# Summing the modulation by rows of 1024 columns instead of 512, with the bias added at the way out of PSUM

## The chip, the cores and the metric

The kernel runs on one core of one Trainium2 chip, as one launch. The metric is the device time of that launch in microseconds (us). The core has five engines with instruction streams of their own: TensorE (PE; its weight loads are shown apart as PEld), VectorE (DVE), ScalarE (ACT), GpSimd (POOL) and SyncE (SP), which here issues nearly all DMAs. PSUM is the memory TensorE writes to; VectorE and ScalarE read results out of it, GpSimd cannot.

## What is computed

Two layers of a diffusion backbone over 512 latent tokens and 256 context tokens, width 1024, all float32. Each layer mixes tokens by three head groups (latent attention, differential attention, a Hyena convolution), then runs a squared-ReLU MLP of width 4096. Both sub-layers are modulated. For each layer the condition vectors are multiplied with a matrix of 1024 x 6144, and the result is cut into six kinds of 1024 numbers:

```
silu_c, silu_cc = jax.nn.silu(c), jax.nn.silu(c_ctx)          # two vectors of 1024
mod   = silu_c  @ w_mod[layer] + b_mod[layer]
mod_c = silu_cc @ w_mod[layer] + b_mod[layer]
sh1, sc1, g1, sh2, sc2, g2 = jnp.split(mod[:, None, :], 6, axis=-1)
px = (layer_norm(x) * (1 + sc1) + sh1) @ w_in[layer]
x  = post_norm(alpha * x + g1 * (ox @ w_out[layer] + b_out[layer]), ...)
x  = post_norm(alpha * x + g2 * ffn(layer_norm(x) * (1 + sc2) + sh2), ...)
```

Kinds 2 and 5 (g1, g2) are gates, one row over all tokens. Kinds 0, 1, 3, 4 are shifts and scales.

## The kernel before

The kernel splits each float32 operand of its large products into a high and a low part and runs three matmuls for each product (`mm3`, `split`). In the MLP, seven of eight blocks of 512 hidden units go through a seven-product (Strassen-like) scheme (`down7`), whose operands are sums made by VectorE or GpSimd and then split again.

Nothing is issued in the order of the program text. Every operation is first recorded as a task (`Plan.note`), with a cost from the kernel's own table (`cost`). `schedule` and `explore` then lay the tasks out in time: in steps of 12 us they try up to 10 orders, nine of them with random changes of the ranks, and keep the one that uses TensorE best over a look ahead. The result is one fixed order for each engine. Where an operation may go to several engines (`either`: `copy` and `scaled` to ScalarE or VectorE, `tt` to VectorE or GpSimd if both inputs are in SBUF, else to VectorE alone; `stt` is VectorE's alone), the planner picks. All instructions go out from line 856, so the profile has one line for everything and the groups are told apart by tile and shape.

SBUF is one arena of 784 units of 64 floats per partition (`S4`, tiles named slab_s in the profile), cut into parts of 16 units. A tile of 512 columns takes 8 units, one of 1024 a whole part. PSUM has eight banks of 512 floats (`mm`, ps_mm in the profile).

Of the twelve kinds of modulation in the two layers, four (layer 0: kinds 0, 1, 3, 4) are multiplied on TensorE by `mod`, which the change leaves alone. The other eight are made by `mod_sum`, without the large matmul: the eight row blocks of 128 rows of `w_mod` are loaded, each multiplied by one number per partition (`cs`, named cc in the profile) and added up in an accumulator of 128 partitions, and at the end a matmul with ones adds the 128 partitions. Layer 0's kinds 2 and 5 and layer 1's kinds 0 and 1 are made for both condition vectors (vs = 2), layer 1's kinds 2 to 5 for the latent tokens' vector alone (vs = 1). `WIDTH` says how many columns are done at a time: with 512, each kind is done in two halves, one after the other.

In each half, the first row block is written to the accumulator by `scaled`, and the bias, loaded to partition 0 alone, is added to partition 0 of it by a `tt` of one partition; the sum over partitions later carries it along. Of the seven other row blocks, those with k + v odd are one `stt` (multiply and add) on VectorE; the others are a `scaled` and a `tt`. At the end a gate's row of 2 x 512 leaves PSUM by `copy` and is written to DRAM (`grow`), to be read back when the gate is used; a shift or a scale lands transposed, 128 x 4 numbers a half, by a `tensor_scalar` into `modT`.

`sums` of layer 0's kind 2 is woven with the spectra of the convolution beside the first projections. The other seven are woven into layer 0's MLP (`RATIO_F`): kind 5 of layer 0 first, then the six of layer 1. Tasks of `mod_sum` are marked loose: the planner's window of 30 us of TensorE work does not wait for them.

Of the kernel before, what the change touches and what calls it, by code (L numbers as in the profile page):

```python
# [12 lines left out]
F32 = mybir.dt.float32  # L13
F32R = mybir.dt.float32r
AF = mybir.ActivationFunctionType
ALU = mybir.AluOpType
AX = mybir.AxisListType
P = 128
# [869 lines left out]
class Net:  # L888
# [7 lines left out]
    DOWN7 = (7, 7)  # L896
    HOT = 12
    UNITS = 784
    WIDTH = 512

    def __init__(self, ctx, tc, A, out):
        self.A, self.out = A, out
# [254 lines left out]
    def mod_sum(self, l, jj, vs):  # L1157

        nc, A = self.nc, self.A
        plan = self.plan  # L1160
        width = self.WIDTH
        n = D // width
        gate = jj in (2, 5)
        if gate:

            g = self.dp.tile([2, D], F32, name=f'grow_{l}_{jj}')
        else:

            t = self.const([P, 8, 2], f'modT_{l}_{jj}')
        for h in range(n):  # L1170
            plan.loose = True
            c0 = jj * D + h * width
            bias = self.S4(width, dt=F32)
            nc.sync.dma_start(out=bias[0:1, :], in_=A['b_mod'][l, c0:c0 + width].unsqueeze(0))
            acc = [self.S4(width, dt=F32) for _ in range(vs)]
            for k in range(8):
                plan.loose = True
                w = self.S4(width, dt=F32)
                nc.sync.dma_start(out=w, in_=A['w_mod'][l, k * P:(k + 1) * P, c0:c0 + width])
                for v in range(vs):  # L1180
                    c = self.cs[:, v, k:k + 1]
                    if k == 0:
                        self.scaled(acc[v], w, c)
                        self.tt(out=acc[v][0:1], in0=acc[v][0:1], in1=bias[0:1], op=ALU.add)
                    elif (k + v) % 2:
                        self.stt(out=acc[v], in0=w, scalar=c, in1=acc[v], op0=ALU.mult, op1=ALU.add)
                    else:
                        x = self.S4(width, dt=F32)
                        self.scaled(x, w, c)
                        self.tt(out=acc[v], in0=acc[v], in1=x, op=ALU.add)  # L1190
                plan.loose = False
                yield 1.0 / n
            plan.loose = True
            if gate:
                row = self.S4(width, dt=F32)
                for o in range(0, width, 512):
                    p = self.mm()
                    for v in range(vs):
                        s = self.pick[:, v] if vs == 2 else self.ones[:, 0:2]
                        nc.tensor.matmul(p[0:2], s, acc[v][:, o:o + 512], start=(v == 0), stop=(v == vs - 1))  # L1200
                    self.copy(row[0:2, o:o + 512], p[0:2])
                nc.sync.dma_start(out=g[:, h * width:(h + 1) * width], in_=row[0:2])
            else:
                m = width // P
                p = self.mm(vs, m, 2)
                for v in range(vs):
                    for k in range(m):
                        nc.tensor.matmul(p[:, v, k], acc[v][:, k * P:(k + 1) * P], self.ones[:, 0:2], start=True, stop=True)
                nc.vector.tensor_scalar(out=t[:, h * m:(h + 1) * m, 0:vs].rearrange('p k v -> p v k'), in0=p[:, :, :, 0],
                                        scalar1=1.0 if jj in (1, 4) else 0.0, scalar2=None, op0=ALU.add)  # L1210
            plan.loose = False
            yield 2.0 / n
        if gate:
            self.grow[l, jj] = g
        else:
            self.modT[l, jj] = t
# [1199 lines left out]
```

## Time and profile before

| | us |
|---|---|
| median of three runs | 1800.85 |
| lowest and highest run | 1797.39, 1802.88 |
| the profiled execution's own time | 1796.01 |
| its span, first to last instruction | 1794.2 |

The profiled execution shows, as shares of the span, PE busy 98%, PEld 83%, DVE 81%, ACT 62%, POOL 29%, with a granted TensorE clock of 0.999 of full speed. An engine's busy time says how long an instruction of its own was in flight. TensorE's matmuls overlap, so its busy time can be near the whole span while the matmuls still come further apart than they could.

### The profile page before, as it was taken

The page shows a single profiled execution, that of the slowest core. Times are in us where ns is not written, and L with a number is a line of the kernel's source. Part 1 is how long each engine was busy: PE and PEld are TensorE (multiplying, and loading weights), DVE is VectorE, ACT ScalarE, POOL GpSimd, SP SyncE. Part 2 cuts the span into 40 slices and gives each one's busy share as a digit, 9 for nine tenths or more (in the row PEclk, how much of TensorE's full clock was granted, in tenths as well). Part 3 has the DMA queues.
Part 4 walks back from the last instruction along what each step waited for, and adds up shares of the span by engine and source line. Part 5 has one row for each costly group of instructions (what it writes and reads, how often), then busy time and mean ns, then how long its engine had stood idle before and what let it go on. Part 6 is the DMA issues. An engine that isn't in the chain of part 4 may idle for free.

```text
span 1794.2 us, 27787 instructions
## 1 busy us (share of the span) xinstructions
PE 1757.7 (98%) x9706; PEld 1480.8 (83%) x9706; DVE 1448.4 (81%) x2554; ACT 1115.2 (62%) x2411; POOL 514.8 (29%) x584
## 2 busy tenths in 40 slices
PE   7999999999999999999999999999999999999997
PEld 2898888887788888887888788998988898888886
DVE  5988866688858999969787788567889788888888
ACT  5645767667828966555554448467679487555542
POOL 3342212174305104214312415012342421222230
PEclk9999999999999999999999999999999999999999
DMA  9497422272334444335334325531524242332251
GB/s 310 88 298 227 137 68 64 83 229 84 121 115 165 165 147 162 105 128 181 103 104 141 135 79 143 193 94 27 185 75 154 91 153 86 119 116 94 94 176 47
DMA packets 165128, 237.21 MB, mean 132 GB/s; under 512 B 36532, under 2 KB 107060, under 8 KB 164987
## 3 DMA queue, kind: packets, MB, share of 16 engines
q1 hardware_dynamic: 153787, 211.84, 36.4%
q0 software_dynamic: 11200, 23.60, 4.4%
q8 instruction: 76, 1.25, 0.3%
q14 instruction: 65, 0.53, 0.1%
HBM read 211.51 MB, written 23.89 MB: 131 GB/s over the span
## 4 chain that ended last, share of the span: by engine, by line
PE 77%; DVE 11%; ACT 6%; DMA 3%; issue 2%; POOL 1%; SPq 0%; POOLq 0%; ACTq 0%; DVEq 0%
PE ps_mm L856 77%; DVE slab_s L856 10%; ACT slab_s L856 6%; DVE st L856 1%; DMA slab_s<-w_mod 1%; DMA slab_s<-w_in 1%; DMA slab_s<-hy_fw 1%; POOL st L856 1%; DMA slab_s<-w_ff 0%; POOL slab_s L856 0%; DMA ident<-k_ident 0%; SPq L856 0%; POOLq L2412 0%; DVE modT L856 0%; ACTq L856 0%
## 5 line engine op out<-in xcount | busy, mean ns | idle before, releaser
L856 PE MATMUL ps_mm<-slab_s,slab_s 128*128 128x512 f32 (+7 forms) x8366 | 1624.5, 350 | 13.4 <-ACT slab_s L856 5.9
L856 PEld LDWEIGHTS ps_mm<-slab_s,slab_s 128*128 128x128 f32 (+3 forms) x8366 | 1353.1, 188 | 226.4 <-ACT slab_s L856 22.7
L856 DVE TENSOR_TENSOR slab_s<-slab_s,slab_s 128x512 fp32r<-128x512 f32 (+9 forms) x898 | 623.5, 736 | 118.0 <-ACT slab_s L856 87.5
L856 ACT CAST slab_s<-slab_s 128x512 fp32r<-128x512 f32 (+8 forms) x837 | 454.4, 581 | 226.1 <-DVE slab_s L856 67.8
L856 POOL TENSOR_TENSOR slab_s<-slab_s,slab_s 128x512 fp32r<-128x512 f32 (+9 forms) x258 | 330.8, 1288 | 793.5 <-DVE slab_s L856 342.3
L856 DVE TENSOR_TENSOR slab_s<-ps_mm,slab_s 128x512 f32<-128x512 f32 (+6 forms) x520 | 316.3, 629 | 85.4 <-PE ps_mm L856 50.2
L856 PE MATMUL ps_mm<-ident,slab_s 128*128 128x128 f32 (+3 forms) x1020 | 177.5, 273 | 7.1 <-ACT slab_s L856 4.6
L856 ACT COPY slab_s<-ps_mm 128x512 f32<-128x512 f32 (+6 forms) x229 | 109.8, 489 | 98.0 <-PE ps_mm L856 88.9
L856 ACT ACTIVATE slab_s<-ps_mm,b 128x256 f32<-128x256 f32 (+2 forms) x176 | 71.8, 450 | 144.2 <-PE ps_mm L856 140.6
L856 PEld LDWEIGHTS ps_mm<-ident,slab_s 128*128 128x128 f32 (+3 forms) x1020 | 122.9, 140 | 35.8 <-ACT slab_s L856 13.5
L856 ACT ACTIVATE slab_s<-ps_mm,st 128x768 f32<-128x768 f32 (+2 forms) x162 | 121.9, 762 | 38.0 <-DVE st L856 14.9
L856 DVE TENSOR_REDUCE st<-ps_mm 128x1 f32<-128x768 f32 (+1 forms) x140 | 117.4, 844 | 26.8 <-PE ps_mm L856 24.1
L856 ACT ACTIVATE slab_s<-slab_s,st 128x96 f32<-128x96 f32 (+2 forms) x86 | 64.1, 747 | 66.5 <-DVE st L856 62.4
L856 DVE SCALAR_TENSOR_TENSOR slab_s<-slab_s,st,slab_s 128x1024 f32<-128x1024 f32 (+3 forms) x84 | 92.0, 1097 | 11.1 <-ACT slab_s L856 6.1
L856 ACT ACTIVATE slab_s<-slab_s,cc 128x512 f32<-128x512 f32 x103 | 72.2, 722 | 20.2 <-DVE slab_s L856 12.2
L856 ACT ACTIVATE slab_s<-slab_s 128x256 f32<-128x256 f32 (+3 forms) x186 | 73.5, 435 | 17.3 <-DVE slab_s L856 16.6
L856 ACT CAST slab_s<-ps_mm 128x512 fp32r<-128x512 f32 (+5 forms) x145 | 70.7, 498 | 20.4 <-PE ps_mm L856 17.0
L856 POOL TENSOR_SCALAR st<-st 128x1 f32<-128x1 f32 (+2 forms) x55 | 23.9, 435 | 196.4 <-ACT slab_s L856 195.2
L856 DVE SCALAR_TENSOR_TENSOR slab_s<-slab_s,cc,slab_s 128x512 f32<-128x512 f32 x80 | 63.2, 803 | 3.1 <-POOL slab_s L856 2.7
L856 POOL TENSOR_TENSOR slab_s<-slab_s 128x256 f32<-128x256 f32 (+1 forms) x39 | 34.4, 890 | 99.8 <-DVE slab_s L856 74.2
L856 PE MATMUL ps_mm<-slab_s,cc 128*2 128x512 f32 x128 | 60.6, 592 | 2.3 <-DMA slab_s<-w_mod 2.3
L856 POOL TENSOR_TENSOR st<-st,mhalf 128x1 f32<-128x1 f32 (+2 forms) x59 | 48.2, 817 | 45.6 <-DVE st L856 41.5
(92 smaller groups left out, 660.6 us busy)
## 6 DMA issues: line engine op xcount, KB each, us to landing
slab_s<-w_ff SPq DMA_DIRECT2D x128, 512.0 KB
slab_s<-w_mod SPq DMA_DIRECT2D x128, 256.0 KB
slab_s<-w_mod SPq DMA_DIRECT2D x32, 512.0 KB
slab_s<-x SPq DMA_DIRECT2D x22, 512.0 KB
slab_s<-w_in SPq DMA_DIRECT2D x24, 384.0 KB
slab_s<-k_fw_l POOLq DMA_DIRECT2D x16, 512.0 KB, 5.3
slab_s<-k_iv_l POOLq DMA_DIRECT2D x16, 512.0 KB, 5.4
slab_s<-w_out SPq DMA_DIRECT2D x16, 512.0 KB
```

The source lines that it names most:

```text
L856: made[i] = f(*[put(v) for v in a], **{n: put(v) for n, v in k.items()})
```

## The change

`WIDTH` goes from 512 to 1024, so each of the eight kinds is done in one pass over whole rows. The bias is no longer added to partition 0 of the accumulator. It is loaded where the result needs it: for a gate on two partitions, 1024 numbers each, and added as the row leaves PSUM (a `tt` in place of `copy`); for a shift or scale as 128 x 8, eight numbers per partition, which are 1024 words of four bytes each from addresses that are 128 words apart along a partition, and added in the `stt` that replaces `tensor_scalar`.

```
-    WIDTH = 512
+    WIDTH = 1024
...
-            bias = self.S4(width, dt=F32)
-            nc.sync.dma_start(out=bias[0:1, :], in_=A['b_mod'][l, c0:c0 + width].unsqueeze(0))
+            b_mod = A['b_mod'][l, c0:c0 + width]
+            if gate:
+                bias = self.S4(width, dt=F32)
+                nc.sync.dma_start(out=bias[0:2, :], in_=b_mod.unsqueeze(0).to_broadcast([2, width]))
+            else:
+                bias = self.S4(width // P, dt=F32)
+                nc.sync.dma_start(out=bias, in_=b_mod.rearrange('(m p) -> p m', p=P))
...
                         self.scaled(acc[v], w, c)
-                        self.tt(out=acc[v][0:1], in0=acc[v][0:1], in1=bias[0:1], op=ALU.add)
...
-                    self.copy(row[0:2, o:o + 512], p[0:2])
+                    self.tt(out=row[0:2, o:o + 512], in0=p[0:2], in1=bias[0:2, o:o + 512], op=ALU.add)
...
-                nc.vector.tensor_scalar(out=t[:, h * m:(h + 1) * m, 0:vs].rearrange('p k v -> p v k'), in0=p[:, :, :, 0],
-                                        scalar1=1.0 if jj in (1, 4) else 0.0, scalar2=None, op0=ALU.add)
+                self.stt(out=t[:, h * m:(h + 1) * m, 0:vs].rearrange('p k v -> p v k'), in0=p[:, :, :, 0], scalar=1.0 if jj in (1, 4) else 0.0,
+                         in1=bias.unsqueeze(1).to_broadcast([P, vs, m]), op0=ALU.add, op1=ALU.add)
```

## Rows read from the trace of the kernel before

**Rows 1.** Windows of the whole core: busy time (instructions) of each engine, clock, DMA

```profile
535.00:960.00 425.00, 421.47 (x2252) 355.27 (x2251) 371.35 (x581) 265.88 (x569) 126.24 (x108) 1.00 0.43 143
140.00:200.00 60.00, 59.84 (x323) 49.99 (x322) 52.84 (x87) 38.24 (x71) 11.84 (x11) 1.00 0.74 229
1500.00:1750.00 250.00, 249.90 (x1098) 204.75 (x1097) 207.24 (x286) 133.03 (x269) 67.31 (x50) 1.00 0.36 116
```

**Rows 2.** Waits of TensorE from 535 to 960 us: total, times, longest

```profile
PE ps_mm L856 <- DVE slab_s L856: 1.8, 1, 1.8
PE ps_mm L856 <- ACT slab_s L856: 0.7, 1, 0.7
PE ps_mm L856 <- POOL slab_s L856: 0.3, 1, 0.3
```

**Rows 3.** The chain of waits, from 589 to 621 us

```profile
589.65 0.77 DVE slab_s L856 x2
...
590.48 2.18 DMA slab_s<-w_mod
592.66 0.63 DVE slab_s L856
...
596.56 8.64 DMA slab_s<-w_mod
605.22 3.56 DMA slab_s<-w_ff
...
609.26 3.46 DVE slab_s L856 x6
```

**Rows 4.** Groups by shape over the span: what the change touches, and nearest shapes

```profile
L856 DVE TENSOR_TENSOR slab_s<-slab_s,slab_s 128x512 f32<-128x512 f32 x190 | 135.2, 737 | 20.8 <-ACT slab_s L856 20.2
...
L856 ACT ACTIVATE slab_s<-slab_s,cc 128x512 f32<-128x512 f32 x103 | 72.2, 722 | 20.2 <-DVE slab_s L856 12.2 <-DMA slab_s<-w_mod 6.8 <-POOL slab_s L856 0.9
...
L856 DVE SCALAR_TENSOR_TENSOR slab_s<-slab_s,cc,slab_s 128x512 f32<-128x512 f32 x80 | 63.2, 803 | 3.1 <-POOL slab_s L856 2.7
...
L856 DVE SCALAR_TENSOR_TENSOR slab_s<-slab_s,st,slab_s 128x1024 f32<-128x1024 f32 x36 | 49.2, 1368 | 10.2 <-ACT slab_s L856 6.1 <-POOL st L856 3.6
L856 DVE SCALAR_TENSOR_TENSOR slab_s<-slab_s,slab_s 128x1024 f32<-128x1024 f32 x36 | 44.1, 1232 | 0.2
...
L856 ACT ACTIVATE slab_s<-slab_s,st 128x1024 f32<-128x1024 f32 x38 | 43.6, 1149 | 51.5 <-DVE st L856 50.5 <-DMA slab_s<-w_mod 0.4 <-PE ps_mm L856 0.3
...
L856 DVE TENSOR_TENSOR slab_s<-slab_s,slab_s 128x1024 f32<-128x1024 f32 x17 | 23.1, 1370 | 0.0
...
L856 DVE TENSOR_TENSOR slab_s<-slab_s,slab_s 1x512 f32<-1x512 f32 x18 | 13.3, 757 | 0.7 <-ACT slab_s L856 0.6
...
L856 ACT COPY slab_s<-ps_mm 2x512 f32<-2x512 f32 x15 | 8.6, 571 | 8.0 <-PE ps_mm L856 7.9
...
L856 DVE SCALAR_TENSOR_TENSOR slab_s<-slab_s,cc 128x512 f32<-128x512 f32 x8 | 6.7, 832 | 0.0
...
L856 POOL TENSOR_TENSOR slab_s<-slab_s,slab_s 1x512 f32<-1x512 f32 x6 | 7.7, 1279 | 5.8 <-DVE slab_s L856 2.9 <-ACT slab_s L856 2.1 <-issue 0.7
```

**Rows 5.** The same view, what reads PSUM on VectorE with a second operand

```profile
L856 DVE TENSOR_TENSOR slab_s<-ps_mm,slab_s 128x512 f32<-128x512 f32 x327 | 215.6, 682 | 56.0 <-PE ps_mm L856 50.2 <-ACT slab_s L856 2.4 <-DMA slab_s<-k_win_c 0.8
```

**Rows 6.** Tiles w_mod, b_mod and grow: issues, shortest/median/longest ns, first and last start

```profile
L856 SPq DMA_DIRECT2D slab_s<-w_mod x160: 327/368/1487, 1.9 to 953.5; - x160
...
L856 SPq DMA_DIRECT2D slab_s<-b_mod x20: 244/272/491, 3.0 to 944.1; - x20
...
L856 SPq DMA_DIRECT2D grow<-slab_s x8: 250/251/257, 172.3 to 1004.4; - x8
L856 SPq DMA_DIRECT2D slab_s<-grow x6: 326/339/459, 465.6 to 1714.5; - x6
```

**Rows 7.** Scattered loads: issue of MLP bias and convolution weights; then windows while they run

```profile
L856 SPq DMA_DIRECT2D b<-b_ff x2: 398/414/430, 62.8 to 1087.9; - x2
...
L856 SPq DMA_DIRECT2D cw<-hy_conv_w x2: 478/1621/2764, 42.4 to 1075.2; - x2
...
60.00:65.00 5.00, 5.00 (x31) 5.00 (x30) 4.97 (x14) 4.85 (x11) 0.00 (x0) 1.00 0.27 6
65.00:70.00 5.00, 5.00 (x25) 4.39 (x25) 4.60 (x10) 1.76 (x4) 2.75 (x5) 1.00 0.26 2
```

**Rows 8.** Matmuls by shape from 690 to 705 us, and from 1500 to 1750 us

```profile
L856 PE MATMUL ps_mm<-slab_s,slab_s 128*128 128x512 f32 x68 | 15.7, 391 | 0.0
...
L856 PE MATMUL ps_mm<-slab_s,slab_s 128*128 128x512 f32 x1098 | 250.5, 390 | 0.1
```

## The prediction

> **What bounds the kernel now.** I read the windows first, then TensorE's waits, then the chain of waits, and only then the prices of single instructions. The windows tell where the touched work lies. The sums load `w_mod` until 953.5 us [rows 6], in two stretches: 140 to 200 us (layer 0, kind 2) and 535 to 960 us (the other seven kinds). In the second TensorE is busy 421.47 of 425 us, in the first 59.84 of 60 [rows 1]. So all the time in which TensorE visibly stands still there is 3.53 + 0.16 = 3.7 us, 0.2% of the kernel. The reader should compare this with VectorE in the same row: 371.35 of 425, 87%, the fullest of the engines that feed TensorE. It is the one that the change relieves, and it is not the one that sets the end, except at a few places.
>
> Which places, the waits tell: from 535 to 960 us TensorE waited 1.8 us for VectorE, 0.7 for ScalarE, 0.3 for GpSimd [rows 2]. The chain of waits shows the worst one, at the start of layer 0's MLP: VectorE, then loads of `w_mod` (2.18 and 8.64 us), one of `w_ff` (3.56) and VectorE's splits again, up to 612.7 us [rows 3]. There the sums' work and the MLP's first weights compete.
>
> **The change, part by part.** A sum of one kind with two vectors has, per half, 2 `scaled` for the first block, 7 `stt`, and 7 `scaled` with 7 `tt`; with one vector 1, 4, 3 and 3. Four kinds of each sort in two halves make 88 `stt`, 104 `scaled` and 80 `tt`, and 24 adds on one partition. The rows have these counts: 80 + 8 `stt`, 103 `scaled` on ScalarE, 18 + 6 adds on one partition [rows 4]. With whole rows the first three halve, and the adds go.
>
> TensorE: the same matmuls. A gate has two slices of 512 columns per vector in either version, a shift or scale eight of 128. Nothing gained or lost here, and no row excludes this since their number follows from the code.
>
> VectorE, `stt`: 63.2 + 6.7 = 69.9 us now [rows 4]. The 44 that remain have 1024 columns. No such instruction with cc is in the trace; the nearest have 1368 ns (a number per partition from st) and 1232 ns (no such number) [rows 4]. So 60.2 or 54.2 us, a saving of 9.7 or 15.7. I take 9.7, since the row with st has the same operands. The `tt` adds: 737 ns for 512 columns and 1370 for 1024 [rows 4] make 40 x 1370 against 80 x 737, so between 0 (all on GpSimd) and 4.2 us saved; I take 2. The adds on one partition: 13.3 us go from VectorE and 7.7 from GpSimd [rows 4]. The gates' way out of PSUM comes over from ScalarE: 8 rows of 2 x 512 at the 682 ns of a `tt` that reads PSUM and SBUF [rows 5], 5.5 us more on VectorE, and 8 x 571 ns = 4.6 less on ScalarE [rows 4]. The four small `stt` that take the place of eight `tensor_scalar` I set at nothing: a fraction of a microsecond each, after the sum, with their readers far away. VectorE in sum: -9.7 - 2 - 13.3 + 5.5 = -19.5 us, with ends at -17.5 and -27.7. ScalarE: 72.2 us become 52 x 1149 ns = 59.7, so -12.5, and with the copies -17 [rows 4].
>
> SP: 64 fewer loads of `w_mod` at 368 ns and 8 fewer of `b_mod` at 272 [rows 6], 26 us of issue time. The bytes are the same, DMA is at 0.43 of its engines in the long stretch [rows 1], so I count nothing.
>
> The bias of a shift or scale becomes 1024 scattered words, in four loads. The nearest load is the MLP's bias, 4096 scattered words issued at 62.8 us: in the two windows from 60 to 70 us the DMA engines are busy 0.27 and 0.26 while moving 6 and 2 GB/s [rows 7]. That is at most 2.65 us of all engines for 4096 words, so 0.66 us for 1024, and 2.7 us for four. Its issue took 0.4 us; that of the convolution's weights, also scattered, once 2.76 against 0.27 for a `b_mod` row [rows 6, 7]: 2.5 us more on SP's queue for each load at worst, 10 in all. Below, nothing: the bias is not needed before the end of its kind, and what is queued behind it on SP is `w_mod` for the same sums and `w_ff`, which mostly arrive with time to spare. I take nothing, and keep 0 to 10 for the range. The Trainium skill, "DMA: Bandwidth & Descriptors", Specifications, says that a transfer needs 512 bytes or more for full rate, and these words have 4. The trace agrees in kind, 6 and 2 GB/s beside 0.27 and 0.26 of the engines [rows 7]; by the rule alone the loads would be slow, and by the row the four of them are 2.7 us.
>
> New waits: the gate's row waits for VectorE rather than ScalarE and holds two PSUM banks until then. Behind it stands only the write of `grow`, and the first read of a gate starts at 465.6 us while the first write starts at 172.3 [rows 6]. If that cover were gone, each of eight evictions would cost some 0.7 us, 5.5 in all. The accumulators take twice the space for twice as long, some 40 units of 784 more for a gate with two vectors; I have no row for what that costs.
>
> So 19.5 us less on VectorE, 17 on ScalarE and 7.7 on GpSimd lie beside TensorE's work, and what can come through is bounded by TensorE's standstill: 0 below, 3.7 above. The 1.8 us for VectorE and the 0.7 for ScalarE [rows 2] are at the place where the relief acts, so I take 2.5. From the profiled execution that is 1796.0 - 2.5 = 1793.5. The median of the runs lies 4.85 us above that execution, so 1798.35 for the median, say 1798.
>
> **The rivals.** *Faster, because TensorE is less full than it looks.* Between 690 and 705 us 68 matmuls of 512 columns start, one each 220.6 ns; from 1500 to 1750 us 1098, one each 227.7 [rows 8]. So TensorE counts as busy while its matmuls come 3% apart more than at best. Over 425 + 60 us this is up to 15 us that a freer VectorE could give back. Against it: the sparse stretch has no sums in it, and VectorE is less busy there (207 of 250) [rows 1], so the spacing is hardly the sums' doing. Half of it, 7.5, with the 2.5 gives 1800.85 - 10 = 1791. The Trainium skill, "Perfetto Trace Analysis", Identifying the Most-Contended Engine, says that TensorE's room is not read from its matmul busy time but from the weight loads' busy share and the useful work. Here that share is 355.27 of 425, 84% [rows 1], which speaks for this rival.
>
> *Slower, by coarser work on VectorE.* A whole-row `stt` holds VectorE 1368 ns where a half held it 803 [rows 4]. Where it stands ahead of a split that TensorE waits for, that comes 0.565 us later; the place is the MLP's start at 575 to 625 us and every block start where the chain runs over VectorE. With the gain of 2.5, it takes 14 of the 44 to be over 0.3% slower (14 x 0.565 = 7.9); with 16 of them 9.0 - 2.5 = 6.5, so 1807. For it: VectorE at 87%. Against: a static order that knows the lengths can put the long ones elsewhere.
>
> *The order as a whole.* All tasks after 140 us are laid out anew, partly by random tries, also where nothing of the sums is left. The rest of the kernel then moves by as much as the order happens to be better or worse, in either direction: several microseconds, about 1794 or 1807. Nothing in the profile says which.
>
> *The scattered loads show.* 2.7 us if each stands ahead of a needed weight load: 1801, no change.
>
> **How the numbers follow.** 0.3%, 5.4 us, is about what a measurement of this kernel can tell from no change. The forecast, the relief mostly hidden, gets 0.42, with a range of its own of 1796 to 1802; the scattered loads, 0.08; both are within 0.3%, in sum 0.50. The faster rival 0.22 and a better order 0.07, in sum 0.29. Coarser work 0.13 and a worse order 0.08, in sum 0.21. The range leaves out about 1 in 10 on either side: 1788, a little beyond the faster rival, and 1808, a little beyond the slower.
>
> **What would show it.** In the profile after: 44 `stt` with cc at 1024 columns near 1.37 us, 52 `scaled` near 1.15, no adds of 1 x 512, VectorE's busy time 17 to 28 us lower and ScalarE's about 17, TensorE's instructions unchanged in number. From 535 to 960 us TensorE's standstill would stay under 3.7 us. The forecast is wrong if TensorE's standstill grows or its matmuls come further apart at the block starts (coarser work), if the stretch without sums, after 1100 us, changes by more than the one with them (the order), or if matmuls of 512 columns come nearer to 220 ns in the stretch of the sums (the faster rival).

## The result, and the profile after

The changed kernel takes 1807.54 us (median of 8 runs, 1804.7 to 1812.55), the kernel before 1799.68 (8 runs, 1796.17 to 1802.88) in the same series. The ratio is 1.0054, 95% interval 1.0043 to 1.0066: slower by half a percent, beyond the 0.3% that counts here. The forecast was 1798 us. The profiled execution has a span of 1803.4 us, 9.2 more than before; its granted clock is 0.996 where that of before has 0.999, so a part of the 9.2 us, at most some 5 (0.003 of the span), is the clock of two single executions.

The page of the profile, busy time of each engine (share of the span) and instructions:

```profile
PE 1763.9 (98%) x9706; PEld 1483.5 (82%) x9706; DVE 1425.3 (79%) x2456; ACT 1094.8 (61%) x2350; POOL 516.3 (29%) x579
```

The windows that answer to [rows 1], and TensorE's waits from 535 to 960 us that answer to [rows 2]:

```profile
535.00:960.00 425.00, 424.00 (x2265) 359.80 (x2264) 339.73 (x491) 251.27 (x521) 113.88 (x90) 1.00 0.40 135
140.00:200.00 60.00, 57.23 (x303) 48.55 (x302) 47.76 (x69) 33.53 (x55) 16.04 (x13) 1.00 0.68 217
1500.00:1750.00 250.00, 249.81 (x1095) 204.23 (x1094) 207.37 (x287) 135.91 (x275) 65.84 (x51) 1.00 0.35 115
```

```profile
PE ps_mm L856 <- DVE slab_s L856: 0.9, 2, 0.7
```

The groups by shape that answer to [rows 4], and the last step of a shift or scale from the view of the tile modT (shortest/median/longest ns, first and last start):

```profile
L856 ACT ACTIVATE slab_s<-slab_s,cc 128x1024 f32<-128x1024 f32 x52 | 59.4, 1152 | 22.9 <-DMA slab_s<-w_mod 10.4 <-POOL slab_s L856 5.1 <-DVE slab_s L856 4.4
L856 DVE SCALAR_TENSOR_TENSOR slab_s<-slab_s,cc,slab_s 128x1024 f32<-128x1024 f32 x44 | 58.7, 1342 | 6.2 <-POOL slab_s L856 5.8 <-ACT slab_s L856 0.3
...
L856 DVE TENSOR_TENSOR slab_s<-ps_mm,slab_s 2x512 f32<-2x512 f32 x8 | 5.3, 671 | 10.8 <-PE ps_mm L856 10.8
```

```profile
L856 DVE SCALAR_TENSOR_TENSOR modT<-ps_mm,slab_s x4: 152/158/170, 695.5 to 945.0; 128x16 f32<-128x16 f32 x2, 128x8 f32<-128x8 f32 x2
```

The reader is to see that everything the change was priced at is there. VectorE is 23.1 us less busy (1448.4 to 1425.3), ScalarE 20.4 (1115.2 to 1094.8), and in the MLP's stretch TensorE stands still 1.0 us where it was 3.53. The kernel is slower all the same, so the loss must lie elsewhere. To find it, each matmul of both traces was given a fixed price for its shape (0.2206 us for 512 columns, [rows 8]; both kernels have the same 9706), and the times were compared at which the same amount of TensorE's work had been started. The amounts 130, 200, 490 and 900 us lie at 151, 225, 534 and 963 us in before. What the changed kernel loses (+) or gains (-) between them, in us:

```
                          to 130  130-200  200-490  490-900   to end    span
after - before               5.2      2.1      3.7     -2.8      0.9     9.2
```

More than half, 5.2 us, is lost by 130 us of work, and 5.1 of it by 120 us of time. In before the first sum's `w_mod` is loaded from 145.6 us on, so the loss is there before any sum is loaded. Windows of the start of before, and then of the changed kernel (columns as in [rows 1]):

```profile
10.00:50.00 40.00, 34.70 (x107) 9.29 (x107) 25.08 (x56) 25.09 (x42) 13.81 (x28) 1.00 1.08 360
50.00:80.00 30.00, 29.22 (x166) 26.73 (x165) 29.41 (x66) 24.72 (x52) 9.90 (x15) 1.00 0.40 54
...
100.00:125.00 25.00, 24.58 (x141) 23.42 (x141) 20.91 (x43) 10.75 (x19) 9.79 (x16) 1.00 1.15 350
```

```profile
10.00:50.00 40.00, 35.71 (x86) 7.42 (x85) 24.19 (x53) 21.45 (x35) 13.41 (x28) 0.91 1.06 346
50.00:80.00 30.00, 28.43 (x174) 26.48 (x174) 27.06 (x65) 23.01 (x47) 17.37 (x15) 1.00 0.47 72
...
100.00:125.00 25.00, 23.21 (x132) 21.31 (x132) 18.44 (x41) 11.28 (x19) 12.66 (x22) 1.00 1.20 334
```

TensorE's waits from 50 to 130 us, before and then after:

```profile
PE ps_mm L856 <- ACT slab_s L856: 1.2, 2, 0.8
```

```profile
PE ps_mm L856 <- ACT slab_s L856: 1.7, 2, 1.6
PE ps_mm L856 <- POOL slab_s L856: 1.6, 1, 1.6
```

From 10 to 50 us the granted clock is 0.91: some 7 of the 40 us went by at 1.2 GHz instead of 2.4, which can make up at most 3.6 us of the loss. After that come a wait of 1.6 us for GpSimd and one of 1.6 for ScalarE that before does not have in that length. No instruction of a sum is near. The lists of instructions of the two programs differ on SyncE from the first DMA, on TensorE from the eleventh instruction.

### The profile page after: what moved, and what is told of

Its sections match the earlier page's. It is cut to its first block, busy times and chain, and to the rows that moved or that the text cites. A ratio compares the mean times of both kernels' runs of the same rounds, so it can differ in the third digit from the quotient of the medians.

```text
span 1803.4 us, 27426 instructions
## 1 busy us (share of the span) xinstructions
PE 1763.9 (98%) x9706; PEld 1483.5 (82%) x9706; DVE 1425.3 (79%) x2456; ACT 1094.8 (61%) x2350; POOL 516.3 (29%) x579
## 5 line engine op out<-in xcount | busy, mean ns | idle before, releaser
L856 PE MATMUL ps_mm<-slab_s,slab_s 128*128 128x512 f32 (+8 forms) x8366 | 1619.3, 350 | 18.9 <-ACT slab_s L856 7.9
L856 DVE TENSOR_TENSOR slab_s<-slab_s,slab_s 128x512 fp32r<-128x512 f32 (+8 forms) x844 | 599.4, 752 | 129.3 <-ACT slab_s L856 92.7
L856 POOL TENSOR_TENSOR slab_s<-slab_s,slab_s 128x512 fp32r<-128x512 f32 (+8 forms) x251 | 332.4, 1330 | 804.6 <-DVE slab_s L856 353.7
L856 DVE TENSOR_TENSOR slab_s<-ps_mm,slab_s 128x512 f32<-128x512 f32 (+8 forms) x528 | 319.6, 629 | 108.9 <-PE ps_mm L856 66.7
L856 PE MATMUL ps_mm<-ident,slab_s 128*128 128x128 f32 (+3 forms) x1020 | 169.8, 273 | 4.4 <-DVE slab_s L856 2.1
L856 ACT COPY slab_s<-ps_mm 128x512 f32<-128x512 f32 (+6 forms) x223 | 104.2, 482 | 90.8 <-PE ps_mm L856 82.7
L856 ACT CAST slab_s<-ps_mm 128x512 fp32r<-128x512 f32 (+4 forms) x146 | 70.1, 497 | 21.1 <-PE ps_mm L856 15.9
L856 ACT ACTIVATE slab_s<-slab_s,cc 128x1024 f32<-128x1024 f32 x52 | 59.4, 1152 | 22.9 <-DMA slab_s<-w_mod 10.4
L856 DVE SCALAR_TENSOR_TENSOR slab_s<-slab_s,cc,slab_s 128x1024 f32<-128x1024 f32 x44 | 58.7, 1342 | 6.2 <-POOL slab_s L856 5.8
L856 POOL TENSOR_TENSOR slab_s<-slab_s 128x256 f32<-128x256 f32 (+2 forms) x38 | 32.8, 871 | 73.2 <-DVE slab_s L856 61.1
```

What stands on the lines that cost most here:

```text
L856: made[i] = f(*[put(v) for v in a], **{n: put(v) for n, v in k.items()})
```

## The experiments

**The theories.** 'Draws': the planner's tries add a random number to the rank of each task, and the numbers are dealt out by place, `rng.uniform(-1.0, 1.0, len(plain))`. The program had 15180 tasks, 524 of them of the sums, and has 14940, 284 of them of the sums. With another length, every task gets another number from the second deal on. So the whole order is drawn anew, from the start. 'Rows': it is the change itself, by whole rows that hold VectorE longer. Without the random numbers, most of the other 14656 tasks have the same rank in both programs: three among the first 30 differ, and 1551 further on, between the pieces of the sums that are woven in, by at most 1.8 us of TensorE's work.

**e1 and e2: the numbers exchanged.** In e1 the changed kernel deals as the kernel before did: it draws 15180 numbers and leaves out those of the sums that are gone. In e2 the kernel before gets the changed kernel's numbers in the same manner.

```
-                rank = ranks if k == 0 else (plain + self.AMP[k % len(self.AMP)] * rng.uniform(-1.0, 1.0, len(plain))).tolist()
+                rank = ranks if k == 0 else (plain + self.AMP[k % len(self.AMP)] * self.noise(rng)).tolist()
...
+    def noise(self, rng):
+        u = rng.uniform(-1.0, 1.0, self.DRAWN)
+        theirs = np.zeros(self.DRAWN, bool)
+        for a, b in self.SUMS_AT:
+            theirs[a:b] = True
+        ours = np.array([t.loose and t.lag == 0.0 for t in self.tasks])
+        out = np.empty(len(ours))
+        out[~ours] = u[~theirs]
+        out[ours] = np.resize(u[theirs], ours.sum())
+        return out
```

> The changed kernel, but every task that both kernels have gets in the planner's random tries the number that it got in the kernel before. Theory 'draws' (the random numbers are drawn for as many tasks as there are, 15180 before and 14940 after, so every task got another number, and the order changed from the first instructions on, which lost 5.1 us by 120 us, before any sum is loaded): the start is that of before, no half-speed spell of the clock between 10 and 100 us, the lag behind before at 100 us of TensorE's work under 0.5 us, the whole 3 to 6 us less than the changed kernel, 1801 to 1805. Theory 'rows' (whole rows hold VectorE longer and that is what costs): the whole stays at 1806 to 1810.

> The kernel before, with the changed kernel's random numbers for every task that both have. Theory 'draws': the start of the changed kernel comes along without its change: half-speed spells of the clock between 10 and 40 us, 4 to 6 us behind before at 100 us of TensorE's work, whole 1803 to 1808. Theory 'rows': no slower than before, 1798 to 1802.

e1 took 1794.95 us, 0.9980 of before (0.9969 to 0.9991): faster than before, where the changed kernel as it stands is slower. e2 took 1804.2 us, 1.0031 (1.0020 to 1.0042): the kernel before, with nothing of the change, becomes slower by numbers alone. e2 lies in the range that 'draws' gave it; e1 lies 6 us below its range of 1801 to 1805, so more came back than the start had lost. Read the other way, the same four kernels say that the changed kernel's numbers cost 0.31% without the change and 0.74% with it, and that the change gives 0.20% with one set of numbers and costs 0.23% with the other. TensorE's first 491 instructions in e1 have the shapes and the order of before. In e2 the first 541 matmuls have those of the changed kernel. TensorE's waits from 50 to 130 us in e1 and then in e2:

```profile
PE ps_mm L870 <- ACT slab_s L870: 1.2, 2, 0.8
```

```profile
PE ps_mm L870 <- ACT slab_s L870: 1.7, 1, 1.7
PE ps_mm L870 <- POOL slab_s L870: 1.6, 1, 1.6
```

The two waits of the changed kernel stand in e2 with their lengths, and e1 has the wait of before. They belong to the numbers and not to the sums. The clock is a part of its own. Windows of e1, then of e2:

```profile
10.00:50.00 40.00, 34.90 (x91) 8.31 (x91) 24.85 (x55) 24.23 (x40) 13.80 (x28) 0.96 1.07 355
```

```profile
10.00:50.00 40.00, 34.34 (x103) 8.58 (x102) 25.82 (x56) 21.49 (x37) 13.41 (x28) 1.00 1.14 356
...
100.00:125.00 25.00, 23.27 (x125) 21.90 (x124) 19.04 (x39) 10.90 (x19) 10.65 (x17) 0.93 1.20 345
```

e1 has the order of before and yet a granted clock of 0.96 there where before had 1.00, and stands 1.7 us behind at 130 us of work. e2 has full clock up to 50 us, against the expectation, and the lower one at 100 to 125, for a start 4.2 us behind before. So the half-speed stretches between 10 and 40 us, expected as a mark of the numbers, were no such mark: e1, which was to be free of them, has one, and e2, which was to have them, has it later. The order's standstills recur with the order; where the clock falls does not. So the 1.7 us of e1, whose matmuls have the order of before there, go with the clock's 0.96 over 40 us (0.04 x 40 = 1.6), and the starts of the changed kernel and of e2 hold such a part too, beside the waits.

**e3 and e4: no random numbers at all.** Both kernels with the plain order alone.

```
-    TRIES, STEP, LOOK, AMP, DENSE = 10, 12.0, 50.0, (3.0, 1.0), 0.985
+    TRIES, STEP, LOOK, AMP, DENSE = 1, 12.0, 50.0, (3.0, 1.0), 0.985
```

> The kernel before, planned with the plain order alone (TRIES 1, so no random number is used). It is the pair of the next run; both theories expect it slower than before by some us, 1800 to 1825.

> The changed kernel with the plain order alone. No draw differs between it and the run before it. Theory 'draws': within 5 us of that run, of either sign, and on VectorE 17 to 28 us less busy. Theory 'rows': 6 to 10 us slower than that run.

1816.05 us (1.0095) and 1814.35 (1.0090): no difference, with VectorE 21.8 us less busy (1449.0 to 1427.2). 'Rows' expected e4 6 to 10 us slower. But e4 shows a place where whole rows do cost. Windows of e3, then of e4, over the first sum:

```profile
140.00:200.00 60.00, 58.29 (x314) 48.56 (x313) 52.23 (x86) 38.71 (x72) 16.71 (x14) 1.00 0.72 229
```

```profile
140.00:200.00 60.00, 56.03 (x288) 46.12 (x287) 48.92 (x64) 33.88 (x56) 18.92 (x14) 0.97 0.72 229
```

TensorE stands still 4.0 us against 1.7, and e4 falls 4.3 us behind e3 there; up to 1.8 of it is the clock, 0.97 in that line.

**e5 to e8: one part at a time, with the numbers of before.** e5 is e1 with the first sum in halves again; e6 has only the first sum in whole rows; e7 has only the new way of the bias; e8 only the whole rows, the bias on partition 0.

```
-        width = self.WIDTH
+        width = 512 if (l, jj) == (0, 2) else self.WIDTH
```

is e5; e6 is `self.WIDTH if (l, jj) == (0, 2) else 512`; e7 is e1 with `WIDTH = 512`; e8 is the kernel before with `WIDTH = 1024` and e1's `noise`.

> e1's kernel (changed kernel, old draws), but the first sum (layer 0, kind 2, beside the projections) again in halves of 512, the other seven in whole rows. Theory 'coarse at the first sum' (with equal draws the changed kernel lost 2 to 4 us between 140 and 200 us in three of four pairs' comparisons so far, with TensorE waiting for VectorE's 1024-column work): TensorE stands still under 1 us between 140 and 200 us (2.1 in e1, 0.2 in before), and the whole is 1 to 3 us less than e1, 1792 to 1794. Rival 'only the order' (the 2 us there are the luck of the re-drawn order): no nearer to before there than e1, the whole 1793 to 1800.

> The reverse: old draws, the first sum in whole rows, the other seven in halves, with the new way of the bias everywhere. Theory 'coarse at the first sum, relief in the MLP': loses 2 to 4 us between 140 and 200 us against before, gains under 2 us from 535 to 960, the whole 1800 to 1804. Rival 'only the order': anything from 1794 to 1806, without that pattern.

> Old draws, the new way of the bias alone, WIDTH 512. It takes 24 adds on one partition (13 us of VectorE, 8 of GpSimd) away. Theory 'VectorE's relief in the MLP': gains 1 to 3 us from 535 to 960 us against before, about two thirds of VectorE's saving being the adds, and nothing at 140 to 200 us; the whole 1796 to 1800. If the scattered loads of the bias cost anything, it shows here, as a loss of up to 3 us.

> Old draws, WIDTH 1024 alone, the bias still added to partition 0 (12 adds of 1 x 1024). Theory 'coarse at the first sum, relief in the MLP': loses 2 to 4 us between 140 and 200 us, gains 1 to 4 from 535 to 960; the whole 1795 to 1801.

| | us | ratio to before (95%) |
|---|---|---|
| e5, first sum in halves | 1802.2 | 1.0020 (1.0010 to 1.0030) |
| e6, first sum alone in rows | 1799.08 | 1.0010 (0.9998 to 1.0023) |
| e7, bias alone | 1797.02 | 0.9997 (0.9987 to 1.0007) |
| e8, rows alone | 1789.6 | 0.9955 (0.9933 to 0.9977) |

The same two windows of e1, e5, e6, e7 and e8, in this order:

```profile
140.00:200.00 60.00, 57.86 (x308) 48.48 (x306) 50.37 (x68) 35.63 (x58) 18.16 (x14) 1.00 0.73 232
...
535.00:960.00 425.00, 424.64 (x2276) 360.37 (x2276) 346.53 (x493) 254.57 (x522) 127.97 (x105) 1.00 0.42 140
```

```profile
140.00:200.00 60.00, 59.93 (x325) 50.34 (x324) 52.80 (x88) 38.33 (x69) 8.12 (x8) 1.00 0.75 229
...
535.00:960.00 425.00, 419.27 (x2234) 354.98 (x2233) 341.18 (x482) 253.39 (x527) 120.50 (x95) 0.99 0.39 134
```

```profile
140.00:200.00 60.00, 57.86 (x313) 48.42 (x312) 50.33 (x70) 36.98 (x61) 18.10 (x14) 1.00 0.71 229
```

```profile
140.00:200.00 60.00, 59.94 (x325) 50.36 (x325) 52.67 (x89) 38.81 (x69) 8.11 (x8) 1.00 0.75 229
```

```profile
535.00:960.00 425.00, 424.10 (x2271) 359.02 (x2270) 358.85 (x502) 262.71 (x542) 123.66 (x100) 1.00 0.42 143
140.00:200.00 60.00, 59.75 (x316) 49.41 (x315) 52.66 (x74) 37.95 (x62) 10.20 (x9) 1.00 0.74 232
```

At the first sum the pattern came as expected for four of the five: TensorE stands still 2.1 us with whole rows (e1, e6) and 0.1 with halves (e5, e7). e8 has whole rows too, and 0.25. For the whole it decides nothing: e5 has the better first sum and is 7 us slower than e1. It lost 9.9 us against e1 between 490 and 900 us of work, where both have the same sums and VectorE is even a little less busy (341.18 and 346.53 us); TensorE's standstill there makes up 5.4 us of it, 5.73 against 0.36, and the clock up to 3 more: it is 0.97 from 600 to 700 us in e5's profile and 1.00 in e1's. So the theory 'coarse at the first sum' fell as an account of the time, and one stretch turned out to swing by ten microseconds between two orders of the same work. The rival 'only the order' gave 1793 to 1800 us for e5 and was missed as well. e6 came 1 us below its range.

e7's whole came as expected, its place did not: a gain of 1 to 3 us from 535 to 960 us was expected from two thirds of VectorE's relief, and TensorE stands still 3.97 us there where before has 3.53. VectorE is 15.3 us less busy in e7, so 0.9997 says that the scattered loads cost no more than that relief gives; it can't part the two. e8, expected at 1795 to 1801, is the fastest kernel of the study, ahead of both kernels compared here, and its way of adding the bias is the dearer one: 11 adds of 1 x 1024 on VectorE, 15.3 us in all, of which the changed kernel has none. That called for other numbers.

**e9 to e16: other numbers for both kernels.** The seed of the draws is changed, and each task that both kernels have gets the same number in both; the sums' tasks draw from a generator of their own.

```
-        rng = np.random.default_rng(0)
+        rng = np.random.default_rng(1), np.random.default_rng(1001)
...
+        out[~ours] = rng[0].uniform(-1.0, 1.0, (~ours).sum())
+        out[ours] = rng[1].uniform(-1.0, 1.0, ours.sum())
```

> The kernel before with other random numbers in the planner's tries (seed 1), nothing else changed. Theory 'draws': its time lies off that of before by as much as the changed kernel's does, 2 to 10 us, of either sign, and the largest part of the difference arises where no sum is at work. Theory 'rows' (the change itself costs the 8 us): within 3 us of before.

> The changed kernel with seed 1, each task that both have with the number that it has in the run before this one. Theory 'draws': within 6 us of that run, of either sign, rather faster; the first 140 us as in that run. Theory 'rows': 6 to 10 us slower than that run.

> The kernel before with seed 2. Theory 'draws': 2 to 10 us off before or off e9, of either sign. Theory 'rows': within 3 us of both.

> The changed kernel with seed 2, paired with the run before this one as above. Theory 'draws': within 6 us of its pair, of either sign, rather faster; the pairs old draws (-4.6), new draws (+3.3 to 3.9), one try (-1.7) and seeds 1 and 2 have a mean between -4 and 0 us. Theory 'rows': 6 to 10 us slower than its pair.

> The kernel before with seed 3. One more drawing of the spread: 'draws' expects 1794 to 1806.

> The changed kernel with seed 3, paired with e13. 'Own effect nil' (the four pairs so far with random draws: -0.20%, +0.09%, +0.11%, +0.23%, mean +0.06%): within 0.3% of e13, either sign. 'Rows': 0.3 to 0.6% slower than e13.

> Whole rows with the bias still on partition 0, seed 1, paired with e9 and e10. Theory 'e8 is luck' (its 1790 us came from its order): within 5 us of e9, 1792 to 1801. Rival 'the old bias is better with whole rows': 6 to 9 us less than e9, 1787 to 1790.

> The same with seed 2, paired with e11 and e12. 'e8 is luck': within 5 us of e11, 1793 to 1803. Rival: 6 to 9 us less than e11, 1789 to 1792.

Ratios to the kernel before, run beside each (e1 to e4, e5 to e8, e9 to e12 and e13 to e16 each shared its runs), the quotient of the pair, and the mean granted clock of the runs behind each ratio:

| numbers | before | changed | changed / before | rows only | clock before | clock changed |
|---|---|---|---|---|---|---|
| of before | 1 | 0.9980 (e1) | -0.20% | 0.9955 (e8) | 0.9962 | 0.9962 |
| of the changed kernel | 1.0031 (e2) | 1.0054 | +0.23% | | 0.9953 | 0.9935 |
| none | 1.0095 (e3) | 1.0090 (e4) | -0.05% | | 0.9962 | 0.9935 |
| seed 1 | 0.9986 (e9) | 0.9995 (e10) | +0.09% | 1.0027 (e15) | 0.9963 | 0.9933 |
| seed 2 | 0.9999 (e11) | 1.0010 (e12) | +0.11% | 1.0013 (e16) | 0.9971 | 0.9944 |
| seed 3 | 0.9976 (e13) | 0.9995 (e14) | +0.19% | | 0.9965 | 0.9946 |

The expectation of e9 and e11, 2 to 10 us off, was too bold for e11: these draws moved the kernel before by 0.14% and 0.01% only, which 'rows' had expected too. The pairs then went against 'rows', which had e10, e12 and e14 clearly slower than theirs. Over its five random draws it spreads from 0.9976 to 1.0031, the changed kernel from 0.9980 to 1.0054. The six quotients have a mean of +0.06% and a standard deviation of 0.16%; a 95% interval for the mean is -0.11% to +0.23%. No effect of the change of its own is seen, and one of 0.5% would lie outside, if the six pairs may stand for all orders. e8's gain was its order's luck: with seeds 1 and 2 whole rows with the old bias came out 0.41% and 0.14% slower than e9 and e11 (e15 a little above its range of 1792 to 1801 us).

**The clock is not the same in the two kernels.** In five of the six pairs the changed kernel ran at a lower mean clock than its partner, in the sixth at the same: 0.0020 less in the mean, with a 95% interval of 0.0009 to 0.0032. Among the runs of one kernel, the time rises by about 1.1 us for each 0.001 that the clock falls (an estimate from 245 runs of all kernels, each kernel's about its own mean). So the lower clock is worth about 2.2 us. Without it the mean of the pairs, +0.06% or 1.1 us, would be about 1 us in favour of the change, by this estimate, with 2.6 us either way. The rows-only kernels e15 and e16 have 0.9933 and 0.9951, e7 with the new bias alone 0.9967, so the lower clock goes with the whole rows and not with the bias; but e1 and e8 have whole rows too, and 0.9962 and 0.9964. Why it is lower is not shown.

By stretches of TensorE's work, in us (the changed kernel less its pair; single profiled executions):

```
                          to 130  130-200  200-490  490-900   to end    span
old numbers, e1 - before     1.7      1.8      0.7     -5.5     -0.3    -1.6
new numbers, after - e2      1.0      0.2      3.2     -6.3      4.0     2.2
one try, e4 - e3            -0.5      4.3     -0.1     -3.6     -4.6    -4.5
seed 1, e10 - e9             0.7     -0.2      0.9     -2.4     -3.2    -4.1
seed 2, e12 - e11           -0.5     -0.2      2.1      0.7     -1.5     0.6
seed 3, e14 - e13           -0.4      1.7      2.6     -2.9      2.0     3.0
mean                         0.3      1.3      1.6     -3.3     -0.6    -0.7
```

The MLP's stretch gains in five of six pairs, 3.3 us in the mean (95% interval 0.7 to 5.9); the two stretches before it lose 1.3 (-0.6 to 3.2) and 1.6 (0.2 to 2.9). At the end, where no sum is left, the pairs differ by -4.6 to +4.0. That is the noise under which the whole lies.

## Why the prediction was wrong

**What was forecast and what came.** The forecast was 1798 us, no change that could be told, with 0.21 for slower. 1807.54 lies just inside the upper end of the range, 1808, and beside the 1807 of 'coarser work on VectorE'. That nearness is luck: the place of that rival was the MLP's start, and no loss is seen there.

**The prices were right.** VectorE was to be 17 to 28 us less busy and is 23.1; ScalarE 17 less and is 20.4. The whole-row `stt` takes 1342 ns (1368 taken), the `scaled` 1152 (1149), the gates' row 671 (682). Only GpSimd's 7.7 us did not come: it is busy 516.3 us after 514.8. The scattered loads were put at nothing, and e7, which has them together with the relief of the adds, shows no cost.

**The 2.5 us at the MLP came as a size.** TensorE's standstill from 535 to 960 us fell from 3.53 to 1.0 us, and by equal work the changed kernel gains 2.8 us there on before; over the six pairs 3.3. That a shorter wait for VectorE is how it comes, as forecast, is not shown by all: the standstill in that stretch fell in four of the six pairs (it grew by 1.0 and 1.2 us with seeds 1 and 2), and e7 has two thirds of the relief without it.

**The step that failed is the term for the order, which the sum had at nothing.** It starts from the profiled execution of before and takes 2.5 us off, as if all else stayed in its place. The order stood beside the sum as the last rival, 'the order as a whole', with 0.08 for a worse one, and was to begin at 140 us: "All tasks after 140 us are laid out anew". It begins near the first instruction, for the numbers are dealt out over the whole program by its length. e2 shows what that term is: with the new numbers and without the change, 1804.2 us against 1799.5, 4.7 us more. e1, with the numbers put back, turns the sign. The sign that was named for the order, a larger change after 1100 us than in the stretch with the sums, did not show it: the last stretch differs by 0.9 us, the start by 5.2.

**The rest, 3.3 us between the changed kernel and e2, holds a second thing that the sum has no term for.** The clock of the changed kernel is 0.0018 lower than that of e2, which is worth about 2 of these 3.3 us by the estimate above. What is left lies within what draws alone do to either kernel.

**'Coarser work on VectorE'** was a rival with its place at the MLP's start. There it did not happen. At the first sum three pairs of six lose 1.7 to 4.3 us by equal work and three gain or lose no more than 0.2, so it is a cost that an order can hide. TensorE's standstill from 140 to 200 us is longer in five of the six, by 1.4 us in the mean. **'TensorE is less full than it looks'** could not be told from the draws.

Open remain three things: why five of six pairs lose between 200 and 490 us of work, where the first sum is over; why the clock is lower with whole rows; and whether the small sums of gains and losses add up to anything. The mean of six pairs can't tell 0.2% from none.

## What to carry to other kernels

Where an order comes from a search with random tries, a change in the number of tasks redraws the whole order, and a difference of half a percent between two single builds says nothing of the change: deal the same numbers to the tasks that both have, compare several seeds, and set the granted clocks beside the times. Look in both traces first at a stretch that the change can't touch. If they differ there, that difference is the yardstick for all the others, and the cheapest gain may be to try more seeds (1793 to 1804 us for the kernel before, 1795 to 1808 for the changed one).

## What the runs showed of the hardware

With the same order of TensorE's first 491 instructions, the granted clock from 10 to 50 us was 1.00 in the profile of before and 0.96 in that of e1, in a stretch where TensorE is busy 34.7 and 34.9 of 40 us and its weight loads 9.29 and 8.31. In the changed kernel it was 0.91, with weight loads busy 7.42 of 40. Over whole runs the changed kernel's mean clock went from 0.996 at 1805.16 us to 0.992 at 1812.55: its spread from run to run, much of which goes with the time at 1.2 GHz, is as large as the effect that was sought. The Trainium skill, "TensorE: Matmul & The Clock Gate", Part 1, says of a kernel's start that the number of matmuls at the low clock varies from run to run of one kernel. The runs here agree in that the mean clock varies, and they add falls in mid-run, as the 0.97 from 600 to 700 us in e5, in a kernel whose TensorE is busy 98% of the span.

One place of such falls is the first sum. From 140 to 200 us the clock is 0.97 in e4 and e14 and 0.94 in e16, all with whole rows there, and each fall lies in or right behind a standstill of TensorE of 2.3, 1.9 and 5.5 us. It is 1.00 in all eight kernels that have the first sum in halves. But it is 1.00 too in the other seven with whole rows, the changed kernel among them, with a wait of 2.6 us. So this is a hint of how whole rows could cost clock, and no more.
